# Two feature tiles of an up-projection by plain block products, other PSUM banks for the first output products, and a last column tile in two banks

## The chip, the cores and the metric

The kernel runs on one core of a Trainium2 chip. The metric is the device time of one execution in microseconds (us). Engines are named as in the profile: PE (TensorE, the matmuls), PEld (its weight loads), DVE (VectorE), ACT (ScalarE), POOL (GpSimd), SP (SyncE, which issues nearly all DMAs here).

## The reference

One decoder layer on 16 meta tokens and 1024 tokens, model width 1024, all in float32:

```
a   = rmsnorm(h) @ w_in                     # 1024 -> 3584: q, k, v of attention; q, f, i, g of HGRN
y1  = differential attention, 4 heads       # softmax(q1 k1) - lam * softmax(q2 k2), T5 bias, causal
y2  = HGRN2, 4 heads                        # gated linear recurrence, rmsnorm, silu gate
h   = h + rmsnorm([y1, y2] @ w_out)         # 1024 -> 1024
u   = causal conv3(rmsnorm(h) @ w_up) + b   # 1024 -> 2 * 2816
out = h + rmsnorm((gelu(u_gate) * u_up) @ w_down)
```

## The kernel before, in words

**Matmuls.** Every float32 matrix is split into a high part in the fast 32-bit format and the rest as a low part; a block product is three matmuls, high times high, high times low and low times high. A split is a cast on ACT and a subtraction on DVE or POOL.

**Order of work.** PE runs its instructions in the order in which the code writes them; generators that yield are interleaved by hand. On ACT, DVE, POOL and SP a scheduler sets the order by data readiness and its own costs, except where the code ties an instruction behind another (`tc.issue_after`, L1165 and others) or asks for program order. Once set, each engine works strictly in that order.

**Stages, with their place in the profile (us).** 0 to 66: norm and first projections. 66 to 538: heads in turn. Attention of head h is interleaved with the projections of HGRN head h, and HGRN head h with the attention projections of head h + 1. Beside them runs a side generator `wd_sums` (L254): first `down_sums`, which forms sums of down-projection weights, then `up_parts` (L214 to 252). It loads the four raw blocks of the up weights of feature tiles 1 and 2, forms the seven Strassen combinations with sums on POOL, splits each (cast on ACT, subtraction on POOL, L224), and stores both parts to a DRAM tensor `usc`: 28 stores of 256 KB.

538 to 602: the last HGRN head is interleaved with the first half of the output products, `out_first` (L1055). HGRN runs there as a recursion of levels; each level needs products of `mix` and `kr` from DVE before PE's next `pl` matmuls (L493). `out_first` goes through token blocks in the order `FIRST` (L960). Its first two blocks take their PSUM banks from `ps_in` (L1056), the pool that the input projections used until then; the last of these, `pi_hg`, is read by DVE to make `gate`. Rows of `w_out` are loaded (`wor`), cast (`woh`) and split (`wol`) by `load_wo`; `mix_split` splits `mix` into `mm` and stores it to `msc`.

602 to 667: second half of the output products, `py1`, a loop over nine token blocks in `order` (L1249 to 1290). In it `post_a` and `post_b` do norm and residual of a block and write its normed row `a2s`; `trans` (L1139) transposes it on PE two blocks later, and ACT copies it to `at2`. Half 0 of the tokens is split into quarter blocks (`t_split`) and Strassen sums (`t_sums`) on the way.

667 to 696: the transition (L1384 to 1425). Feature tile 0 goes through `plain_unit` (L1322): for each half of the tokens four quarters of 24 matmuls, that is two column blocks times two sides (gate `ug`, up `uu`), each over two inner blocks of four. The first two quarters of half 0 have a PSUM bank each, the third and fourth share one two-bank tile of attention's (`ps_s("pq2")`). Each quarter is read by an ACT copy. Then `gated` does convolution (`conv`, `c`), GELU and product.

696 to 1112: feature tiles 1 to 21 go through `unit` (L1342): seven Strassen products of 12 matmuls for each half of the tokens, PSUM accumulators `pa`, `pb`, `pc`. `prep(q)` (L1202) makes the weights of product q; for tiles 1 and 2 it loads them from `usc`, from tile 3 on it loads four raw blocks, sums on POOL and splits.

1112 to 1340: down-projection, in seven Strassen steps (`steps`, L1506 on), and the tail. The last column tile of the last product (m = 3) is cut into two halves of 256 in `last_sum_halves` (L1580), both in the bank `banks[4][3]`: matmuls of a half, addition to `x1`, squares; then rstd, two gains (`last_out`) and the output DMAs.

Of the kernel before, what the change touches and what calls it, by code (L numbers as in the profile page):

```python
# [18 lines left out]
P = 128  # L19
# [3 lines left out]
D = 1024  # L23
# [63 lines left out]
def layer_kernel(ctx: ExitStack, tc: tile.TileContext, x, meta, table, lbl, gpre, gpost, win,  # L87
# [56 lines left out]
    usc = dp.tile([2, 7, 2, P, 512], F32, tag="usc", name="usc")  # L144
# [22 lines left out]
    def rstd_of(dst, ss, n):  # L167
        A.activation(dst, ss, AF.Ln, bias=eps[: dst.shape[0]], scale=1.0 / n)
        A.activation(dst, dst, AF.Exp, scale=-0.5)
# [44 lines left out]
    def up_parts():  # L214
        b = [wsp.tile([P, 512], F32, tag="wd", name=f"up{n}") for n in range(5)]

        def load(ft, **what):
            for n, nm in what.items():
                with tc.issue_after(last_load[-1].ins):
                    SY.dma_start(b[int(n[1])], up_raw(ft, nm))  # L220

        def out(ft, j, src):
            A.copy(b[2].bitcast(F32R), src)
            G.tensor_tensor(b[3].bitcast(F32R), src, b[2], op=ALU.subtract)  # L224
            for l in range(2):
                with tc.issue_after(last_load[-1].ins):
                    SY.dma_start(usc[ft - 1, j, l], b[2 + l])

        load(1, b0="21", b1="22", b4="11")
        yield  # L230
        for ft in (1, 2):
            G.tensor_tensor(b[0], b[0], b[1], op=ALU.add)
            out(ft, 2, b[0])
            yield
            G.tensor_tensor(b[0], b[0], b[4], op=ALU.subtract)
            out(ft, 1, b[0])
            yield
            out(ft, 5, b[1])
            load(ft, b1="12")
            yield  # L240
            G.tensor_tensor(b[0], b[1], b[0], op=ALU.subtract)
            out(ft, 6, b[0])
            load(ft, b0="21")
            yield
            out(ft, 4, b[1])
            yield
            out(ft, 0, b[4])
            yield
            G.tensor_tensor(b[0], b[4], b[0], op=ALU.subtract)
            out(ft, 3, b[0])  # L250
            if ft == 1:
                load(2, b0="21", b1="22", b4="11")
            yield

    wd_sums = chain(down_sums(), up_parts())
# [799 lines left out]
    def out_first():  # L1055
        pys = [ps_in(f"py0_{i}") for i in FIRST[:2]]  # L1056
# [48 lines left out]
    a2t, xhs, a2s = {}, {}, []  # L1105
# [6 lines left out]
    def post_a(i, py):  # L1112
# [9 lines left out]
        V.scalar_tensor_tensor(xh[:r, 512:], tmp[:r], s1, xh[:r, 512:], ALU.mult, ALU.add)  # L1122

    def post_b(i):
# [8 lines left out]
        rstd_of(s2, s2, D)  # L1133
        V.scalar_tensor_tensor(a2[:r], xh[:r], s2, gfb[:r], ALU.mult, ALU.mult)
# [4 lines left out]
    def trans(i, bank=ps_m):  # L1139
# [4 lines left out]
        for half in range(2):  # L1144
# [4 lines left out]
            A.copy(at2[p][:, 4 * half:4 * half + 4, c:c + r], pt[:, : 4 * r].rearrange("p (k t) -> p k t", k=4))  # L1149
# [8 lines left out]
    def t_split(p, j, src, where, tag, step=None):  # L1158
# [5 lines left out]
        A.copy(hi[:, :, o:], src)  # L1164
        V.tensor_tensor(lo[:, :, o:], src, hi[:, :, o:].bitcast(F32), op=ALU.subtract)  # L1165
        if o:
            for a, b in zip((hi, lo), tt[p][0]):
                A.copy(a[:, :, :o], b[:, :, :o].bitcast(F32))
        tt[p][j] = (hi, lo)
# [20 lines left out]
    def load_raw4(ft, s):  # L1190
        raws.clear()
        for nm in ("11", "22", "21", "12"):
            raws[nm] = swp.tile([P, 512], F32, tag="ra", name=f"ra{s}_{nm}", bufs=5)
            with tc.issue_after(last_load[-1].ins):
                SY.dma_start(raws[nm], up_raw(ft, nm))
# [6 lines left out]
    def prep(q):  # L1202
# [7 lines left out]
        if ft < 3:  # L1210
            for l, t in enumerate((hi, lo)):
                with tc.issue_after(last_load[-1].ins):
                    SY.dma_start(t.bitcast(F32), usc[ft - 1, j, l])
            return
# [20 lines left out]
    def prep_plain():  # L1235
        load_raw4(0, "p")
        for j, nm in enumerate(("11", "12", "21", "22")):
# [11 lines left out]
    for n, i in enumerate(order):  # L1249
# [37 lines left out]
        if i == 8:  # L1287
            prep(8)
# [420 lines left out]
```

## Time and profile before

| what | us |
|---|---|
| median of 3 runs (lowest, highest) | 1345.74 (1342.92, 1347.78) |
| profiled execution | 1341.52 |
| its span, first to last instruction | 1339.7 |
| PE busy | 1286.7 (96%) |
| DVE, ACT, POOL busy | 916.5, 690.0, 424.1 |
| DMA moved | 168.29 MB |
| mean granted clock of TensorE | 0.997 |

Rows of the timeline read: start in us, duration in us, engine, line, operation, output <- inputs (buffer numbers left out), form, count; in brackets the idle time of the engine before it and what ended it. Line L54 stands for the helper that records all ACT and DVE operations, so tiles tell those apart. Rows of a window read: stretch, its length, then busy us and count for PE, PEld, DVE, ACT and POOL, the granted clock, the DMA share and GB/s. Rows of the waits read: engine, line, what it waited for, total us, times, longest.

### The profile page before, as it was taken

The page shows a single profiled execution, that of the slowest core. Times are in us where ns is not written, and L with a number is a line of the kernel's source. Part 1 is how long each engine was busy: PE and PEld are TensorE (multiplying, and loading weights), DVE is VectorE, ACT ScalarE, POOL GpSimd, SP SyncE. Part 2 cuts the span into 40 slices and gives each one's busy share as a digit, 9 for nine tenths or more (in the row PEclk, how much of TensorE's full clock was granted, in tenths as well). Part 3 has the DMA queues.
Part 4 walks back from the last instruction along what each step waited for, and adds up shares of the span by engine and source line. Part 5 has one row for each costly group of instructions (what it writes and reads, how often), then busy time and mean ns, then how long its engine had stood idle before and what let it go on. Part 6 is the DMA issues. An engine that isn't in the chain of part 4 may idle for free.

```text
span 1339.7 us, 26379 instructions
## 1 busy us (share of the span) xinstructions
PE 1286.7 (96%) x10182; PEld 1184.5 (88%) x10182; DVE 916.5 (68%) x1595; ACT 690.0 (52%) x1669; POOL 424.1 (32%) x335
## 2 busy tenths in 40 slices
PE   6999999999998999999989999999999999999997
PEld 5898899989987989777789999999999998888886
DVE  7565657574758465744896777777787776697586
ACT  7465346534653575535674454454454444554453
POOL 3211212021225430103223566666657640010020
PEclk9999999999999999999999999999999999999999
DMA  6331333143314420825844222223222225965353
GB/s 215 108 133 52 104 116 110 48 128 103 103 60 143 134 95 16 261 88 196 268 161 154 95 74 82 83 77 114 80 88 71 80 80 182 336 205 165 95 205 118
DMA packets 92580, 168.29 MB, mean 126 GB/s; under 512 B 10483, under 2 KB 20755, under 8 KB 92454
## 3 DMA queue, kind: packets, MB, share of 16 engines
q1 hardware_dynamic: 92454, 166.60, 37.4%
q8 instruction: 80, 1.31, 0.4%
q14 instruction: 46, 0.38, 0.1%
HBM read 120.56 MB, written 46.01 MB: 124 GB/s over the span
## 4 chain that ended last, share of the span: by engine, by line
PE 53%; DVE 6%; ACT 3%; issue 2%; DMA 2%; POOL 1%; SPq 0%; DVEq 0%; ACTq 0%; POOLq 0%
PE pd L1527 5%; PE pd L1528 5%; PE pd L1526 5%; PE pb L1355 4%; PE pb L1356 4%; PE pb L1357 4%; PE pa L1355 2%; PE pa L1356 2%; PE pa L1357 2%; PE pc L1356 2%; PE pc L1355 2%; PE pc L1357 2%; PE py L1012 2%; PE py L1016 2%; PE py L1014 2%
## 5 line engine op out<-in xcount | busy, mean ns | idle before, releaser
L1355 PE MATMUL pb<-t,uh 128*128 128x258 f32 (+1 forms) x504 | 142.6, 283 | 2.1 <-DVE u L54 1.9
L1357 PE MATMUL pb<-t,ul 128*128 128x258 f32 (+1 forms) x504 | 141.4, 281 | 0.0
L1356 PE MATMUL pb<-t,uh 128*128 128x258 f32 (+1 forms) x504 | 141.3, 280 | 0.0
L1526 PE MATMUL pd<-wh,gh 128*128 128x512 f32 (+1 forms) x307 | 120.9, 394 | 1.0 <-DVE x L54 1.0
L1527 PE MATMUL pd<-wl,gh 128*128 128x512 f32 (+1 forms) x307 | 121.1, 394 | 0.3 <-DVE wl L54 0.2
L1528 PE MATMUL pd<-wh,gl 128*128 128x512 f32 (+1 forms) x307 | 121.0, 394 | 0.0
L1319 POOL TENSOR_TENSOR c<-c,c 128x512 f32<-128x512 f32 x44 | 63.0, 1432 | 150.5 <-ACT c L54 129.0
L54 DVE SCALAR_TENSOR_TENSOR c<-uu,cwt,c 128x512 f32<-128x512 f32 x88 | 93.6, 1063 | 20.8 <-ACT c L54 20.1
L1355 PEld LDWEIGHTS pb<-t,uh 128*128 128x128 f32 x504 | 95.1, 189 | 3.3 <-DVE u L54 3.1
L1357 PEld LDWEIGHTS pb<-t,ul 128*128 128x128 f32 x504 | 95.6, 190 | 0.0
L1356 PEld LDWEIGHTS pb<-t,uh 128*128 128x128 f32 x504 | 94.9, 188 | 0.0
L1355 PE MATMUL pa<-t,uh 128*128 128x258 f32 (+1 forms) x336 | 94.7, 282 | 0.0
L1356 PE MATMUL pa<-t,uh 128*128 128x258 f32 (+1 forms) x336 | 94.4, 281 | 0.0
L1357 PE MATMUL pc<-t,ul 128*128 128x256 f32 x336 | 94.3, 281 | 0.0
L1355 PE MATMUL pc<-t,uh 128*128 128x256 f32 x336 | 94.3, 281 | 0.0
L1356 PE MATMUL pc<-t,uh 128*128 128x256 f32 x336 | 94.3, 281 | 0.0
L1357 PE MATMUL pa<-t,ul 128*128 128x258 f32 (+1 forms) x336 | 94.1, 280 | 0.0
L54 DVE SCALAR_TENSOR_TENSOR c<-ug,cwt,c 128x512 f32<-128x512 f32 x88 | 84.5, 960 | 1.8 <-ACT c L54 1.1
L1527 PEld LDWEIGHTS pd<-wl,gh 128*128 128x128 f32 x307 | 57.9, 189 | 14.2 <-DVE wl L54 1.1
L1526 PEld LDWEIGHTS pd<-wh,gh 128*128 128x128 f32 x307 | 57.9, 189 | 14.2 <-DVE x L54 1.2
L1528 PEld LDWEIGHTS pd<-wh,gl 128*128 128x128 f32 x307 | 57.9, 189 | 13.1
L54 ACT ACTIVATE pb<-S,ast 128x528 f32<-128x528 f32 (+7 forms) x72 | 46.5, 647 | 39.0 <-DVE ast L54 38.9
(417 smaller groups left out, 4165.8 us busy)
## 6 DMA issues: line engine op xcount, KB each, us to landing
ra<-in_wup_dram SPq DMA_DIRECT2D x76, 256.0 KB, 2.7
wd<-in_wdown_dram SPq DMA_DIRECT2D x44, 256.0 KB, 4.4
tsc<-wd SPq DMA_DIRECT2D x44, 256.0 KB, 3.1
gsc<-c SPq DMA_DIRECT2D x44, 256.0 KB, 2.0
wi<-tsc SPq DMA_DIRECT2D x44, 256.0 KB, 2.7
gi<-gsc SPq DMA_DIRECT2D x33, 256.0 KB, 4.0
wi<-in_wdown_dram SPq DMA_DIRECT2D x33, 256.0 KB, 3.4
usc<-up SPq DMA_DIRECT2D x28, 256.0 KB, 2.1
```

Of the source, the lines that this page charges most:

```text
L54: ins = call(*args, **kw)
L1012: T.matmul(py[:r], mh[:, j, :r], hi, start=(first and j == 0), stop=False)
L1014: T.matmul(py[:r], mh[:, j, :r], lo, start=False, stop=False)
L1016: T.matmul(py[:r], ml[:, j, :r], hi, start=False, stop=(last and k == k1 - 1))
L1319: G.tensor_tensor(cg, cg, cu, op=ALU.mult)
L1355: T.matmul(pt, hi[:, s], th[:, k], start=(first and k == 0), stop=False, skip_group_check=True)
L1356: T.matmul(pt, hi[:, s], tl[:, k], start=False, stop=False, skip_group_check=True)
L1357: T.matmul(pt, lo[:, s], th[:, k], start=False, stop=(k == 3), skip_group_check=True)
L1526: T.matmul(py, gh[:, s], wh, start=(k == 0 and pr not in (3, 7)), stop=False, skip_group_check=True)
L1527: T.matmul(py, gh[:, s], wl, start=False, stop=False, skip_group_check=True)
L1528: T.matmul(py, gl[:, s], wh, start=False, stop=(k == NH - 1), skip_group_check=True)
```

## The change

It has three parts.

1. `up_parts` and `usc` are gone. Feature tile 1 goes through `plain_unit` too, on weights that `prep_plain(1, ...)` loads and splits near the end of the `py1` loop (splits on POOL). Tile 2 is prepared in place from raw blocks, whose loads are tied behind the first store of unit 0. The transition is written in a new order: splits and sums are moved, and `behind(...)` ties some to marked instructions (`xh`, `rstd`, `turned`, `hi`, `lo`). In the `py1` loop `trans` moves from the third part to the fourth.
2. The first two blocks of `out_first` take banks of attention's pool `ps_s` in place of `ps_in`.
3. The last column tile has two banks, one for each half, and all its steps run as two 256-wide products; the gain of block 2 moves between the halves, and its output DMA goes out in two halves.

```diff
@@ up weights split ahead @@
-    def up_parts():
-        b = [wsp.tile([P, 512], F32, tag="wd", name=f"up{n}") for n in range(5)]
...
-    wd_sums = chain(down_sums(), up_parts())
+    wd_sums = down_sums()
@@ out_first @@
-        pys = [ps_in(f"py0_{i}") for i in FIRST[:2]]
+        pys = [ps_s(f"py0_{i}")[:, 0] for i in FIRST[:2]]
@@ ties @@
+    @contextmanager
+    def behind(*names):
+        with ExitStack() as st:
+            for nm in names:
+                st.enter_context(tc.issue_after(marks[nm].ins))
+            yield
@@ load_raw4 @@
-            with tc.issue_after(last_load[-1].ins):
+            with tc.issue_after(marks["store"].ins if "store" in marks else last_load[-1].ins):
@@ prep @@
-        if ft < 3:
-            for l, t in enumerate((hi, lo)):
-                with tc.issue_after(last_load[-1].ins):
-                    SY.dma_start(t.bitcast(F32), usc[ft - 1, j, l])
-            return
@@ plain weights @@
-    def prep_plain():
-        load_raw4(0, "p")
...
+    def prep_plain(ft, names):
+        for nm in names:
+            raw = swp.tile([P, 512], F32, tag="ra", name=f"rap{ft}_{nm}", bufs=5)
+            with tc.issue_after(last_load[-1].ins):
+                SY.dma_start(raw, up_raw(ft, nm))
+            where = wp if nm[1] == "1" else swp
+            hi, lo = (where.tile([P, 512], F32R, tag=t, name=f"u{t[1]}{ft}_{nm}", bufs=4) for t in ("wh", "wl"))
+            split(hi, lo, raw, G)
+            plain[ft, nm] = (hi, lo)
@@ py1 loop @@
-                if n >= 2:
-                    trans(order[n - 2])
+            if c == 3 and n >= 2:
+                trans(order[n - 2])
...
-            prep(7)
-        if i == 8:
-            prep(8)
+        if i == 3:
+            prep_plain(1, ("12", "22"))
         post_a(i, py)
     post_b(8)
+    with behind("rstd"):
+        prep_plain(1, ("11", "21"))
@@ transition @@
-    p0 = plain_unit(0, lambda nm: free.pop(0))
+    p0 = plain_unit(0, 0, lambda nm: free.pop(0))
+    next(p0)
+    with behind("xh"):
+        t_split(1, 0, quarter(1, 0), tp, "t1_0")
     next(p0)
     trans(7)
-    t_split(0, 1, sum_quarter(0, 1), tp, "t0_1", 264)
-    t_split(0, 2, sum_quarter(0, 2), tp, "t0_2")
-    t_split(1, 0, quarter(1, 0), tp, "t1_0")
-    prep(9)
     next(p0)
-    t_split(1, 4, quarter(1, 4), tp, "t1_4")
-    next(p0)
-    prep(10)
+    with behind("xh", "rstd"):
+        t_split(1, 4, quarter(1, 4), tp, "t1_4")
     next(p0)
     trans(8)
     t_split(1, 7, quarter(1, 7), tp, "t1_5")
     t_split(1, 6, quarter(1, 6), mxp, "mix2", 384)
-    t_split(0, 3, sum_quarter(0, 3), tp, "t0_3")
-    t_split(0, 5, sum_quarter(0, 5), mxp, "mix0", 272)
+    next(p0)
+    with behind("hi", "lo"):
+        t_split(0, 1, sum_quarter(0, 1), tp, "t0_1", 264)
+        t_split(0, 2, sum_quarter(0, 2), tp, "t0_2")
+        t_split(0, 3, sum_quarter(0, 3), tp, "t0_3")
...
+    p0 = plain_unit(1, 0, ps_b)
+    for j in range(4):
+        next(p0)
...
+    p1 = plain_unit(1, 1, ps_b)
...
-    for ft in range(1, NF):
+    for ft in range(2, NF):
@@ last column tile @@
-        py, wh, wl = banks[pr][m][:, c0:c1], wh[:, c0:c1], wl[:, c0:c1]
+        py, wh, wl = (banks[pr][m + c0 // 256] if c1 - c0 < 512 else banks[pr][m])[:, :c1 - c0], wh[:, c0:c1], wl[:, c0:c1]
...
-            V.tensor_tensor(c[:, h], py[:, h], c[:, h], op=ALU.add)
+            if n:
+                last_out(m - 1, 0)
+            V.tensor_tensor(c[:, h], pys[n][:, :256], c[:, h], op=ALU.add)
...
-            mms(i, m)
+            if (pr, m) == (4, 3):
+                mms(i, m, 0, 256)
+                mms(i, m, 256, 512)
+            else:
+                mms(i, m)
```

DVE at the first output products, before: `wol` are low parts of rows of `w_out` for the first half, `wl_0` and `wl_1` rows 0 and 1 for the second half, `mm_0` and `mm_4` low parts of `mix` blocks, `mix` with `f` the products of HGRN level 1.

```order
719 L54 TENSOR_TENSOR wol_6_6455<-wor_6_6452,woh_6_6454 128x512
720 L54 TENSOR_TENSOR wol_7_6461<-wor_7_6458,woh_7_6460 128x512
721 L54 TENSOR_TENSOR mm_0_6558<-mix_101,mm_0_6558 128x512
722 L54 TENSOR_TENSOR mix_101<-mix_101,f_5515 128x384
723 L54 TENSOR_TENSOR mix_100<-mix_100,f_5515 128x272
724 L54 TENSOR_TENSOR mix_102<-mix_102,f_5515 128x384
725 L54 TENSOR_TENSOR a_6488<-pd_6491,ident_729 128x256
726 L54 TENSOR_TENSOR am<-pd_6491,ident_729 16x16
727 L54 TENSOR_TENSOR wl_0_6617<-wor_0_6614,wh_0_6616 128x512
728 L54 TENSOR_TENSOR wl_1_6623<-wor_1_6620,wh_1_6622 128x512
729 L54 TENSOR_TENSOR mm_4_6627<-mix_101,mm_4_6627 128x384
730 L54 TENSOR_TENSOR wol_2_6747<-wor_2_6744,woh_2_6746 128x512
```

The same place in the changed kernel (tile numbers are shifted):

```order
719 L53 TENSOR_TENSOR wol_6_6375<-wor_6_6372,woh_6_6374 128x512
720 L53 TENSOR_TENSOR mm_0_6478<-mix_100,mm_0_6478 128x512
721 L53 TENSOR_TENSOR wol_7_6381<-wor_7_6378,woh_7_6380 128x512
722 L53 TENSOR_TENSOR mix_99<-mix_99,f_5477 128x272
723 L53 TENSOR_TENSOR mix_100<-mix_100,f_5477 128x384
724 L53 TENSOR_TENSOR mix_101<-mix_101,f_5477 128x384
725 L53 TENSOR_TENSOR a_6408<-pd_6411,ident_728 128x256
726 L53 TENSOR_TENSOR am<-pd_6411,ident_728 16x16
727 L53 TENSOR_TENSOR mm_4_6547<-mix_100,mm_4_6547 128x384
728 L53 TENSOR_TENSOR wl_0_6537<-wor_0_6534,wh_0_6536 128x512
729 L53 TENSOR_TENSOR mix_100<-mix_100,f_5477 128x192
730 L53 TENSOR_TENSOR mm_0_6609<-mix_100,mm_0_6609 128x512
```

`mm_0` now stands ahead of `wol_7`, and `wl_1` and `wol_2` have moved behind the products of the next level.

SP's queue of DMAs at the same place, before: `wor` are loads of rows of `w_out`, `msc` stores of split `mix` blocks, `mp` loads of them.

```order
226 L972 DMA wor_0_6614<-in_wout_dram 128x512
227 L972 DMA wor_1_6620<-in_wout_dram 128x512
228 L972 DMA wor_2_6744<-in_wout_dram 128x512
229 L1050 DMA mp_0_6939<-msc 128x512
230 L1050 DMA mp_1_6941<-msc 128x512
231 L1003 DMA msc<-mm_0_6558 256x1x256 x2
```

And in the changed kernel:

```order
188 L929 DMA wor_0_6534<-in_wout_dram 128x512
189 L960 DMA msc<-mm_0_6478 256x1x256 x2
190 L929 DMA wor_1_6540<-in_wout_dram 128x512
191 L960 DMA msc<-mm_4_6547 256x1x256
192 L960 DMA msc<-mm_4_6547 256x1x128
193 L929 DMA wor_2_6664<-in_wout_dram 128x512
```

The loads of rows 1 and 2 of the second half stand behind stores of `mm_0` and `mm_4`, which wait for DVE.

ACT at the transition, before: `t_` are casts of quarter blocks, `at_1` with `pa` the copies of transposed blocks, `ug` and `uu` with `pq` the evacuations of quarters, `c` the convolution and GELU.

```order
763 L54 ACTIVATE at_1_7234,ssy<-xh_7732 128x8x128
764 L54 CAST t_3_8016<-at_0_7238 128x1024
765 L54 ACTIVATE ssy<-ssy,eps 128x1
766 L54 ACTIVATE ssy<-ssy 128x1
767 L54 COPY ug_0_7862<-pq_7859 128x258
768 L54 COPY uu_0_7863<-pq_7860 128x258
769 L54 COPY ug_0_7862<-pq_7861 128x256
770 L54 ACTIVATE c_0_0_8156<-ug_0_7862,cbt,cwt 128x512
771 L54 COPY ug_1_8030<-ug_0_7862 128x2
772 L54 CAST t_5_8019<-at_0_7238 128x4x258
773 L54 ACT_TABLE_LOAD
774 L54 ACTIVATE c_0_0_8156<-c_0_0_8156 128x512
```

And in the changed kernel, up to the evacuation of the fourth quarter:

```order
741 L53 COPY at_1_7154<-pa_7_0_7853 128x4x128
742 L53 ACTIVATE ssy<-ssy,eps 128x1
743 L53 COPY at_1_7154<-pa_7_1_7859 128x4x128
744 L53 ACTIVATE ssy<-ssy 128x1
745 L53 CAST uh_11_7770<-rap_11_7768 128x512
746 L53 CAST uh_21_7776<-rap_21_7774 128x512
747 L53 CAST t_4_7890<-at_1_7154 128x1024
748 L53 COPY ug_0_7798<-pq_7795 128x258
749 L53 COPY uu_0_7799<-pq_7796 128x258
750 L53 COPY ug_0_7798<-pq_7797 128x256
751 L53 COPY uu_0_7799<-pq_7797 128x256
```

The fourth quarter's evacuation (`uu_0<-pq_7861` before, `uu_0<-pq_7797` now) stood behind the table load and GELU and stands ahead of them now. The copies of block 7 and the casts of `uh_11`, `uh_21` and `t_4` stand ahead of the evacuations of the first three quarters.

More of the change, by code (lines that the diff above doesn't have):

```diff
@@ L1 @@
 import math
[L2 to L3 removed]
+from contextlib import contextmanager, ExitStack, nullcontext
 import concourse.bass as bass
@@ L1338, in plain_unit @@
                 yield
-        gated(0, p, *us)
+        with behind("turned"):
+            gated(ft, p, *us)
         yield
```

110 lines of the change are left out of this document (37 added, 73 removed).

## The prediction

> **What bounds the kernel now.** I read the head of the page first, then the chain that ended last, then the waits of PE, and then the stretches in which those waits lie.
>
> ```profile
> span 1339.7 us, 26379 instructions
> PE 1286.7 (96%) x10182; PEld 1184.5 (88%) x10182; DVE 916.5 (68%) x1595; ACT 690.0 (52%) x1669; POOL 424.1 (32%) x335
> PE 53%; DVE 6%; ACT 3%; issue 2%; DMA 2%; POOL 1%; SPq 0%; DVEq 0%; ACTq 0%; POOLq 0%
> ```
>
> TensorE (PE) is busy 96% of the span, and no other engine comes near. Whatever the change is worth must therefore come out of the 53 us in which PE did nothing, out of stretches at a low granted clock, or out of the number of matmuls. The waits of PE say who ends its idle time (total us, times, longest):
>
> ```profile
> PE pl L493 <- DVE mix L54: 7.7, 8, 2.7
> PE pa L1148 <- DVE a2s L54: 3.2, 3, 2.0
> PE py L1012 <- DVE gate L54: 2.6, 2, 2.1
> PE pq L1334 <- ACT uu L54: 2.0, 1, 2.0
> PE pq L1334 <- ACT ug L54: 0.5, 1, 0.5
> PE pd L1526 <- DVE x L54: 1.0, 1, 1.0
> ```
>
> These six rows name every wait that the change touches: HGRN levels that wait for VectorE (DVE), the first output products that wait for a PSUM bank (gate), the transition between output projection and up-projection (a2s, ug, uu), and the last column tile (x). They hold 17 us together, and the change reaches only a part.
>
> **D. Weights no longer split ahead (up_parts goes).** Its DVE, ACT and POOL work lay beside attention and HGRN. The windows compare each stretch "attention projections beside an HGRN head" of heads 0, 1 and 2, and then the three later stretches "HGRN projections beside attention" (length, then busy us of PE, PEld, DVE, ACT, POOL):
>
> ```profile
> 142.90:195.70 52.80, 50.59 (x733) 47.49 (x732) 34.93 (x79) 22.23 (x63) 9.56 (x12) 1.00 0.35 108
> 272.39:326.55 54.16, 51.08 (x733) 47.65 (x732) 34.97 (x79) 22.24 (x63) 10.29 (x12) 1.00 0.33 105
> 403.50:460.80 57.30, 51.06 (x732) 47.47 (x732) 37.75 (x71) 27.12 (x72) 27.49 (x25) 1.00 0.42 137
> 195.70:272.39 76.69, 74.22 (x506) 71.24 (x505) 44.91 (x104) 44.57 (x134) 12.59 (x11) 1.00 0.27 90
> 326.55:403.50 76.95, 74.66 (x506) 71.22 (x506) 46.01 (x104) 45.10 (x135) 16.94 (x14) 1.00 0.29 97
> 460.80:538.57 77.77, 74.38 (x505) 71.16 (x504) 45.67 (x103) 48.44 (x145) 17.81 (x14) 1.00 0.24 79
> ```
>
> Head 2 does the same work as head 0 and 1 plus most of up_parts, and takes 3.14 us longer than head 1 and 4.50 longer than head 0. POOL has 17 us more there, ACT 5. The last stretch, with the rest of up_parts, is 0.82 longer than the one before it and 1.08 longer than the first. Why DVE suffers is seen from one operation of the HGRN head, in the window of head 2 and then of head 1, and from what ran beside it (count, busy us, mean ns):
>
> ```profile
> L224 POOL TENSOR_TENSOR up<-up,up 128x512 fp32r<-128x512 f32 x9 | 12.6, 1399 | 11.8 <-ACT up L54 8.9 <-DMA usc<-up 3.0
> L54 DVE TENSOR_TENSOR kr<-kr,tt 128x520 f32<-128x520 f32 x2 | 3.4, 1680 | 0.0
> ...
> L54 DVE TENSOR_TENSOR kr<-kr,tt 128x520 f32<-128x520 f32 x2 | 1.4, 700 | 0.0
> ```
>
> The same DVE product took 1680 ns beside the splits and 700 without, and the HGRN levels on PE wait for exactly these products (the row "pl <- DVE mix", 7.7 us). With up_parts gone head 2 should look like heads 0 and 1. The gain is 3.1 to 4.5 there plus 0.8 to 1.1 behind. I take the means, 3.8 + 0.95, and round down to **−4.4** because a part of up_parts also ran beside stretches with slack; bounds −3.0 and −5.6. The weights' loads and 28 stores of 256 KB went with it; DMA had room there (share 0.42), so they add nothing.
>
> [...]
>
> **A. First output products in attention's banks.** At 538 us PE changes from the last projection to these products. Rows of PE, ACT, DVE, then the DMA loads of the output weights, and the window:
>
> ```profile
> 542.85 0.50 PE L1012 MATMUL py<-wh,mm 128*128 128x512 f32 x1 [2.10 <-DVE gate L54]
> 545.29 0.63 PE L1014 MATMUL py<-wol,mm 128*128 128x512 f32 x1
> 545.72 0.63 PE L1016 MATMUL py<-woh,mm 128*128 128x512 f32 x1
> 552.79 0.70 PE L493 MATMUL pl<-mix,kr 128*32 128x16 f32 x62
> ...
> 556.43 0.71 PE L493 MATMUL pl<-mix,kr 128*32 128x16 f32 x62
> ...
> 544.19 1.27 ACT L54 CAST woh<-wor 128x512 fp32r<-128x512 f32 x2 [2.16 <-DMA wor<-in_wout_dram]
> ...
> 544.84 1.34 DVE L54 TENSOR_TENSOR wol<-wor,woh 128x512 fp32r<-128x512 f32 x2 [2.05 <-ACT woh L54]
> ...
> DMA to landing us min/median/max: 2.4/4.2/5.6
> ...
> 548.00:564.00 16.00, 16.00 (x334) 12.42 (x333) 13.43 (x34) 7.60 (x15) 3.59 (x5) 1.00 0.93 297
> ```
>
> Both waits for gate (2.6 us) are waits for a bank of the projections, and go. Behind the longer one the matmuls start 0.43 us apart (545.29 to 545.72) where this width otherwise starts every 0.23 (twice the 20.00 us / 172 of the 256-wide ones in the window under B); some eight of them at the half clock lose 1.7 us. The upper bound of A is 2.6 + 1.7 = 4.3.
>
> What is late next is the split of wo row 6 (ready at 545.5: the first of two DVE splits of 0.67 us from 544.84). PE reaches its first product with it after 30 matmuls of 0.23 and the first HGRN level, at 538.6 + 7.6 = 546.2, so it just fits. Level 1 of HGRN (552.79 before) would start at 548.4, once DVE has done row 6, one mm low part, row 7 and three products of mix. That is the full 4.3. But the order on DVE and on the loads' queue moves too: the stores of mix now stand ahead of the second half's weight loads, and wl_1 and wol_2 stand behind them on DVE. A load takes 4.2 us to land in a stretch whose DMA share is 0.93. Going through DVE's order with these durations I get level 2 at 553 (before 556.4), and, each later level a few tenths longer than before, a lead that shrinks to 2.6 by the fifth. I take **−2.6**, bounds −4.3 and 0.
>
> [...] Here a gap of 2.10 us, with 0.5 us just ahead of it, was followed by half-clock spacing, while the one of 2.7 us in the row of pl was not (clock 1.00 in its window). [...]
>
> **B. The transition.** The first matmul of unit 0, the three waits, and the windows of a plain unit (96 matmuls) and of a Strassen tile (168; x172 includes neighbours):
>
> ```profile
> 666.79 0.28 PE L1334 MATMUL pq<-t,uh 128*128 128x258 f32 x1
> ...
> 685.03 0.38 PE L1334 MATMUL pq<-t,uh 128*128 128x256 f32 x1 [1.99 <-ACT uu L54]
> ...
> 685.00:696.00 11.00, 10.97 (x96) 10.97 (x97) 10.49 (x10) 9.26 (x14) 0.00 (x0) 1.00 0.24 64
> 696.00:716.00 20.00, 20.00 (x172) 19.94 (x171) 12.31 (x21) 6.06 (x13) 2.96 (x2) 1.00 0.76 267
> ...
> 670.48 1.28 DVE L54 SCALAR_TENSOR_TENSOR a2s<-xh,ssy,gfb 128x1024 f32<-128x1024 f32 x1
> ...
> 677.01 2.32 DVE L54 SCALAR_TENSOR_TENSOR a2s<-xh,ssy,gfb 128x1024 f32<-128x1024 f32 x1
> ...
> 678.67 0.37 ACT L54 COPY ug<-pq 128x256 f32<-128x256 f32 x1 [1.18 <-PE pq L1336]
> ...
> 684.87 1.08 ACT L54 COPY at<-pa 128x512 f32<-128x512 f32 x2
> 685.83 2.96 ACT L54 CAST t<-at 128x1024 fp32r<-128x1024 f32 x3
> ```
>
> Tile 1 by plain products costs 24 more matmuls of 0.116 us (20.00 / 172): **+2.8**. Three waits stand against it: 2.0 for a2s of block 7, 0.5 for ug, 2.0 for uu, 4.5 together. The first goes because sums and splits of half 0 no longer stand on DVE ahead of a2s; the third because the table load and GELU no longer stand on ACT ahead of the evacuation. The bound without waits is 2.8 − 4.5 = −1.7.
>
> I do not think all goes. Quarters 3 and 4 still share one PSUM tile, so quarter 4 waits for the evacuation of quarter 3. On ACT there now stand ahead of it: two copies of the transposes of block 7 (1.08), the casts of the new weights 11 and 21 (2 x 0.63 by the cast row of A), a cast of t1_4 (1.0, a third of 2.96), and the evacuations of quarters 1 and 2 (2 x 0.37, as the one at 678.67). Counted from unit 0's start, quarters 1 and 2 end at 5.6, the transposes at 6.4, quarter 3 at 9.2. ACT starts the copies at 6.4 at the earliest and has quarter 3 out at 6.4 + 1.1 + 1.3 + 1.0 + 0.7 + 0.4 = 10.9. Quarter 4 waits 1.7. So B is 2.8 − 4.5 + 1.7 = **0.0**. Bounds: −1.7 (ACT free in time), +1.5 (block 6's transposes wait longer, since three sums now stand on DVE ahead of its a2s, or the POOL splits stretch a2s as 677.01 against 670.48: 2.32 for 1.28). Cover: tile 2's weights are loaded after the first store of unit 0 and needed, by my count, some 20 us later, when both units of tile 1 are done (2 x 11.0); a load, a cast and a split are 4.2 + 0.6 + 0.7 of that. If that cover were gone, a first split late by 3 us would cost 3.
>
> **C. The last column tile.** PE's last wait, DVE's last gain, and the last two output DMAs:
>
> ```profile
> 1331.03 0.38 PE L1526 MATMUL pd<-wh,gh 128*128 128x256 f32 x1 [0.96 <-DVE x L54]
> ...
> 1335.41 0.75 DVE L54 SCALAR_TENSOR_TENSOR hh<-x,ssd,hh 128x512 f32<-128x512 f32 x1
> 1335.52 0.99 SPq L1602 DMA_DIRECT2D out_dram<-hh  x2
> ```
>
> With a bank of its own the second half no longer waits for the first half to be read: 0.96 goes. The chain behind (sum, squares, rstd, two gains, two DMAs) keeps its length; only one gain of block 2 changes places, into DVE time in which it waited for PE. The first steps of this tile run as two 256-wide matmuls each, seven steps of three pairs, at 2 x 0.116 for 0.23: +0.1 at most. **−0.9**, bounds 0 and −1.4.
>
> **Sum.** −4.4 − 2.6 + 0.0 − 0.9 = −7.9. The profiled run took 1341.52 (span 1339.7 and 1.8 around it), which is 0.3% under the median of the three runs, 1345.74. I carry the difference over: 1341.5 − 7.9 = 1333.6 on the scale of that run, 1345.7 − 7.9 = **1337.8** on that of the medians, which is what I predict.
>
> **Rivals.**
>
> 1. *The waits only change places.* The stretch of A is bound by its DMA (share 0.93), so that an earlier start buys nothing once the loads are behind the stores (A = −0.5), and ACT's new queue keeps PE waiting in B while block 6 waits too (B = +1.5). D at its lower bound and C stay: −3.0 − 0.5 + 1.5 − 0.9 = −2.9, 1342.8. For it speaks the moved order of SP; against it that PE is the busy engine of 548 to 564 (16.00 of 16.00). Chance 0.15.
> 2. *All terms at their good end.* −5.6 − 4.3 − 1.7 − 1.4 = −13.0, 1332.7. For it: level 1 does start 4.3 earlier in my replay. Against: wl_1's load. Chance 0.18.
> 3. *Slower: weight loads of the second half one level late.* If DVE reaches wl_1 or wol_2 before the load has landed, everything behind it on DVE stands, the level's kr and mix products too, and so PE. The loop is then closed: a mix low part on DVE (0.7) lets the store go, the store lets the load go (1.2 for both issues), it lands 4.2 later, cast and split take 0.63 + 0.67, the level's products 1.7: 9.1 us a level, where levels lie 3.6 apart (552.79 to 556.43). Three such levels lose 16 us, and with the −7.9 that is +8, 1354. It decides from the point at which a load lands more than about 2 us behind DVE. Chance 0.06.
> 4. *The change does not remove its waits.* The banks of S are still held when the first products want them, or quarter 4's wait brings the half clock with it: A = 0, B = +1.5, with D and C as forecast −3.8, 1341.9. Chance 0.08.
>
> The forecast, within its bounds, keeps 0.53.
>
> **How the numbers follow.** A measurement here can tell about 0.3% (4 us) from no change: faster is below 1341.7, slower above 1349.8. The forecast and rival 2 are faster, rivals 1 and 4 mostly within 4 us, rival 3 slower. The forecast's bounds lie nearly all below 1341.7; of rivals 1 and 4, which stand just above it, I count a third as faster. That gives 0.53 + 0.18 + 0.08 = 0.79 faster, 0.15 the same, 0.06 slower. The range takes rival 2 with 1.5 us below it and reaches up to rivals 1 and 4 with 1 us above: 1331 to 1344; rival 3 and some of the extremes stay out.
>
> **What would show it.** Right: head 2's stretch near 53.5 us with kr products at 700 ns; no wait of py for gate, no 0.43 us spacing near 544, level 1 of the last head at 548.4 less what D took ahead of it; a wait of pq for ug of 1.5 to 2 us; no wait of pd for x at the end. Wrong: head 2 still near 57 us (then POOL was not the cause), levels of the last HGRN head more than 5 us apart, a wait of pa for a2s of 2 us, or a wait for tile 2's first weights.

## The result, and the profile after

The changed kernel takes 1336.8 us (median of 6 runs, 1335.2 to 1338.1) against 1345.6 of the kernel before: ratio 0.9937, 95% interval [0.9922, 0.9952], faster by 0.6%. The forecast was 1337.8. Timed again beside the last experiments it took 1338.1, ratio 0.9945 [0.9927, 0.9963]. One execution of experiment 9, the one that was profiled, ran at a mean clock of 0.56 and took 2092.9 us; it is left out.

The page of the changed kernel and the waits of PE (lines have moved by about 40):

```profile
span 1335.8 us, 26319 instructions
PE 1288.8 (96%) x10227; PEld 1191.1 (89%) x10227; DVE 914.6 (68%) x1589; ACT 690.3 (52%) x1670; POOL 414.1 (31%) x324
...
PE pb L1319 <- DVE u L53: 8.1, 4, 6.3
PE pl L450 <- DVE mix L53: 4.9, 7, 1.1
PE pa L1112 <- DVE a2s L53: 2.4, 1, 2.4
PE pq L1297 <- ACT ug L53: 1.4, 1, 1.4
```

PE is busy 2.1 us longer (24 more matmuls) and idle 6 us less (47.0 in place of 53.0). The waits for gate, for uu and for x at the end are gone. The wait of `pl` for mix has fallen from 7.7 to 4.9. One wait is new and large: 6.3 us of `pb` for `u`, in the first Strassen tile.

Where the time went is read from the start of each stage's first matmul. The lengths come from one profile of before and two of the changed kernel, in us; each is a difference of two start times:

| stage | before | changed | changed, second profile |
|---|---|---|---|
| start to attention of head 2 (the same instructions) | 326.55 | 329.05 | 326.32 |
| attention 2 to first output product (D) | 212.53 | 201.63 | 201.39 |
| first output product to HGRN level 5 (A) | 28.87 | 26.03 | 26.29 |
| level 5 to first plain unit | 98.84 | 100.20 | 100.35 |
| first plain unit to tile 2 (B) | 49.06 | 48.31 | 48.31 |
| tile 2 | 19.85 | 28.41 | 28.55 |
| tile 3 to the last matmul (C) | 597.01 | 595.59 | 595.65 |

The first row is a gauge: 330 us of the same instructions take 2.7 us more or less in two profiles of one kernel. In these two profiles the other rows repeat within 0.3 us, but that is not so for all of them in more profiles. The runs of experiments 2, 5 to 8, 10 and 11 have the same instructions in the same order up to level 5: over all nine profiles D is 201.4 to 202.5, and A 26.0 to 28.8. With the old banks A is 28.9 (before) and 30.3 (experiment 4). So the row of D can be taken as it stands, and the row of A only as a mean of several profiles.

The rows behind the first sum to −6.0 and −5.6, while the medians differ by 8.8. The profiled execution of before took 1341.5 against a median of 1345.6, so 2 to 3 us of the gain in time have no place in the table.

D, in the windows of the changed kernel: head 0 and head 1 beside attention projections, attention of head 2 beside HGRN projections, head 2, then the last projections beside attention:

```profile
144.07:196.86 52.79, 50.56 (x732) 47.47 (x732) 34.90 (x79) 22.23 (x63) 9.56 (x12) 1.00 0.33 108
...
274.07:329.05 54.98, 52.37 (x733) 49.17 (x733) 35.07 (x79) 22.24 (x63) 10.41 (x12) 0.97 0.32 104
...
329.05:404.77 75.72, 73.89 (x505) 71.20 (x505) 44.57 (x104) 44.59 (x134) 12.58 (x11) 1.00 0.26 88
404.77:455.99 51.22, 50.57 (x732) 47.54 (x732) 29.19 (x71) 22.23 (x63) 9.56 (x12) 1.00 0.12 37
455.99:530.68 74.69, 73.34 (x506) 71.24 (x506) 44.40 (x102) 47.25 (x140) 9.77 (x8) 1.00 0.12 38
```

Head 2 did not come down to 53.5 as forecast but to 51.22, below heads 0 and 1; the last stretch fell from 77.77 to 74.69. The third busy time (DVE) says why: 29.19 in head 2, 34.90 in head 0. The group behind the difference, in head 0's window of the changed kernel:

```profile
L53 DVE TENSOR_TENSOR wd<-wd,wd 128x512 f32<-128x512 f32 x8 | 5.6, 697 | 2.3 <-DMA wd<-in_wdown_dram 1.4 <-DMA wr_hi<-in_win_dram 0.8
```

Heads 0 and 1 carried eight subtractions of `down_sums` each, 5.6 us of DVE. They were no free baseline: PE's waits in head 0 and in head 2 of the changed kernel, the second of which has one row,

```profile
PE pl L450 <- DVE mix L53: 1.6, 2, 1.0
PE pi_dv L231 <- ACT k L53: 0.5, 1, 0.5
```

```profile
PE pi_dv L231 <- ACT k L53: 0.5, 1, 0.5
```

differ by the 1.6 us by which head 0 is longer. Head 2 before had these, and its `kr` products, 1680 ns before, are short now:

```profile
PE pl L493 <- DVE mix L54: 4.2, 4, 2.7
PE pl L487 <- DVE kr L54: 1.0, 1, 1.0
```

```profile
L53 DVE TENSOR_TENSOR kr<-kr,tt 128x520 f32<-128x520 f32 x2 | 1.4, 698 | 0.0
```

So 5.2 of the 6.1 us in head 2 are waits of the HGRN levels for DVE. In that window of before, eight DVE products took 1.35 to 1.79 us that take 0.29 to 0.74 now, and an operation of POOL overlaps each of them in the trace. No run takes away POOL's part of `up_parts` alone; that POOL and not the transfers slowed DVE rests on these rows.

A: the first output product follows the last projection 0.18 us later, and the levels start at

```profile
530.68 0.40 PE L969 MATMUL py<-wh,mm 128*128 128x512 f32 x1
...
540.48 0.29 PE L450 MATMUL pl<-mix,kr 128*32 128x16 f32 x13
...
556.71 0.27 PE L450 MATMUL pl<-mix,kr 128*32 128x16 f32 x9
```

Against the first product, level 1 comes at +9.80 (before 552.79 − 539.08 = +13.71) and level 5 at +26.03 (before +28.87): a lead of 3.9 that shrinks to 2.8, plus the first wait of 0.5. The lead is lost at one place, between levels 2 and 3. ACT's cast of row 2 of the second half (`woh`) waits there for its load, and DVE stands idle until the cast is done, with the products of level 3 behind it:

```profile
546.15 0.62 ACT L53 CAST woh<-wor 128x512 fp32r<-128x512 f32 x1 [2.63 <-DMA wor<-in_wout_dram]
546.81 0.69 DVE L53 TENSOR_TENSOR wol<-wor,woh 128x512 fp32r<-128x512 f32 x1 [2.37 <-ACT woh L53]
```

Level 3 comes 4.8 us behind level 2 here, against 3.7 before. In the eleven profiles with the new banks DVE's idle time at this place is 2.2 to 3.6 us, and level 3 comes 4.6 to 6.0 us behind level 2, in nine of them more than 5.

The new wait, on PE and then on DVE ahead of it:

```profile
720.18 0.58 PE L1319 MATMUL pb<-t,uh 128*128 128x256 f32 x1 [6.31 <-DVE u L53]
720.57 0.41 PE L1320 MATMUL pb<-t,uh 128*128 128x256 f32 x1
720.78 0.41 PE L1321 MATMUL pb<-t,ul 128*128 128x256 f32 x1
720.99 0.42 PE L1319 MATMUL pb<-t,uh 128*128 128x256 f32 x1
```

```profile
697.78 3.48 DVE L53 SCALAR_TENSOR_TENSOR c<-ug,cwt,c 128x512 f32<-128x512 f32 x2
701.18 2.32 DVE L53 TENSOR_TENSOR t<-at,t 128x1032 fp32r<-128x1032 f32 x1
703.42 2.58 DVE L53 SCALAR_TENSOR_TENSOR c<-uu,cwt,c 128x512 f32<-128x512 f32 x2
705.92 5.69 DVE L53 TENSOR_TENSOR t<-at,t 128x1024 fp32r<-128x1024 f32 x3
711.53 1.78 DVE L53 TENSOR_TENSOR ul<-ra,uh 128x512 fp32r<-128x512 f32 x1
713.23 2.55 DVE L53 SCALAR_TENSOR_TENSOR c<-ug,cwt,c 128x512 f32<-128x512 f32 x2
...
719.71 0.42 DVE L53 TENSOR_TENSOR u<-pb,x 128x256 f32<-128x256 f32 x1
```

PE stands still from 713.9 and then starts matmuls every 0.21 us in place of 0.116 for 4 us: the half clock (granted clock 0.50 from 717.81 to 724.64), about 2 us more. DVE is busy with one gap of 0.27 us: convolutions of tiles 0 and 1, five token splits, three subtractions for tile 2's weights, and only then the addition that frees a PSUM bank. A split of 1.22 us takes up to 2.32 there.

C: DVE at the end of the changed kernel,

```profile
1329.09 0.75 DVE L53 SCALAR_TENSOR_TENSOR hh<-hh,ssd,hh 128x512 f32<-128x512 f32 x1
1329.75 0.42 DVE L53 TENSOR_TENSOR x<-pd,x 128x256 f32<-128x256 f32 x1
...
1331.97 0.74 DVE L53 SCALAR_TENSOR_TENSOR hh<-x,ssd,hh 128x512 f32<-128x512 f32 x1
```

No wait of PE for x is left in this stage. The last addition now starts 0.5 us behind PE's last matmul, held up by the gain of block 2 (0.04 before), but the last gain ends 3.5 us behind that matmul (1329.2), as before (1336.2 behind 1332.7).

### The profile page after: what moved, and what is told of

Its sections match the earlier page's. It is cut to its first block, busy times and chain, and to the rows that moved or that the text cites. A ratio compares the mean times of both kernels' runs of the same rounds, so it can differ in the third digit from the quotient of the medians.

```text
span 1335.8 us, 26319 instructions
## 1 busy us (share of the span) xinstructions
PE 1288.8 (96%) x10227; PEld 1191.1 (89%) x10227; DVE 914.6 (68%) x1589; ACT 690.3 (52%) x1670; POOL 414.1 (31%) x324
## 5 line engine op out<-in xcount | busy, mean ns | idle before, releaser
L1319 PE MATMUL pb<-t,uh 128*128 128x258 f32 (+1 forms) x480 | 136.9, 285 | 8.1 <-DVE u L53 8.1
L1320 PE MATMUL pb<-t,uh 128*128 128x258 f32 (+1 forms) x480 | 135.6, 283 | 0.0
L1321 PE MATMUL pb<-t,ul 128*128 128x258 f32 (+1 forms) x480 | 135.6, 283 | 0.0
L1280 POOL TENSOR_TENSOR c<-c,c 128x512 f32<-128x512 f32 x44 | 66.9, 1520 | 132.0 <-ACT c L53 123.6
L1319 PEld LDWEIGHTS pb<-t,uh 128*128 128x128 f32 x480 | 91.6, 191 | 9.2 <-DVE u L53 8.9
L1321 PEld LDWEIGHTS pb<-t,ul 128*128 128x128 f32 x480 | 92.0, 192 | 0.0
L1320 PEld LDWEIGHTS pb<-t,uh 128*128 128x128 f32 x480 | 91.4, 190 | 0.0
L1319 PE MATMUL pa<-t,uh 128*128 128x258 f32 (+1 forms) x320 | 90.2, 282 | 0.0
L1320 PE MATMUL pa<-t,uh 128*128 128x258 f32 (+1 forms) x320 | 89.9, 281 | 0.0
L1321 PE MATMUL pc<-t,ul 128*128 128x256 f32 x320 | 89.9, 281 | 0.0
L1319 PE MATMUL pc<-t,uh 128*128 128x256 f32 x320 | 89.9, 281 | 0.0
L1320 PE MATMUL pc<-t,uh 128*128 128x256 f32 x320 | 89.9, 281 | 0.0
L1321 PE MATMUL pa<-t,ul 128*128 128x258 f32 (+1 forms) x320 | 89.7, 280 | 0.0
L155 POOL TENSOR_TENSOR ul<-ws,uh 128x512 fp32r<-128x512 f32 x40 | 58.2, 1454 | 35.4 <-ACT uh L53 31.6
```

What stands on the lines that cost most here:

```text
L155: (eng or G).tensor_tensor(lo, raw, hi.bitcast(F32), op=ALU.subtract)
L1280: G.tensor_tensor(cg, cg, cu, op=ALU.mult)
L1319: T.matmul(pt, hi[:, s], th[:, k], start=(first and k == 0), stop=False, skip_group_check=True)
L1320: T.matmul(pt, hi[:, s], tl[:, k], start=False, stop=False, skip_group_check=True)
L1321: T.matmul(pt, lo[:, s], th[:, k], start=False, stop=(k == 3), skip_group_check=True)
```

## Experiments

Ratios are against the kernel before, timed beside each run; the changed kernel has 0.9937 and 0.9945. Runs are compared with the changed kernel by these ratios or by medians. Stretches of the experiments are, like those of the table, from one profile each. The diffs are excerpts; `...` marks what is left out.

**1. up_parts back.** The changed kernel with the removed generator (its text as before, not shown) running, its results unread:

```diff
-    wd_sums = down_sums()
+    wd_sums = chain(down_sums(), up_parts())
```

> The changed kernel with up_parts back beside attention and HGRN: loads, sums, casts, splits and the 28 stores run as before, but nothing reads what they store; everything else is as changed (time 1336.8). Forecast: up_parts costs 4.4 us, so about 1341. Reading of the two profiles (heads 2 and 3 together are 9 to 11 us shorter than before, of which the same instructions ahead of them vary by 2.5): 8 to 10 us, so about 1345 to 1347. If the shorter stretches come from something else, 1337.

Measured: 1349.4 us, ratio 1.0031 [1.0016, 1.0045]. The difference to the changed kernel is 0.9% or 12 us, above both expectations (the upper one, 8 to 10 us, lies at the edge of the intervals). Head 2 and the last stretch in this run:

```profile
405.48:463.06 57.58, 51.10 (x732) 47.48 (x732) 37.79 (x71) 27.12 (x72) 27.46 (x25) 1.00 0.41 136
463.06:540.56 77.50, 74.18 (x505) 71.33 (x505) 45.49 (x102) 48.27 (x144) 17.80 (x14) 1.00 0.23 78
```

They are 6.4 and 2.8 us longer than in the changed kernel, and 11.1 are lost by the first plain unit (667.97 against 656.91), of which 1.9 come between head 3 and there or ahead of head 2. This settles that D is the removal and what it is worth: without it, the rest of the change is slower than before by 0.3%. PE's waits in head 2 are back as they were before: 4.2 us for mix and 1.0 for kr.

**2. Tile 2 with casts only.**

```diff
+        if ft == 2:
+            if j == 0:
+                load_raw4(ft, ft)
+            made[q] = (hi, hi)
+            A.copy(hi, raws[("11", "22", "21", "12")[j % 4]])
+            return
```

> The changed kernel with the preparation of tile 2 cut down: each of its seven products takes one raw block, cast on ACT, as high and as low part, so the POOL sums and the five DVE or POOL subtractions for tile 2 are left out and the output is not the layer's; loads, casts and matmuls stay. If preparing tile 2 in place causes the new wait of 6.3 us at 720 and the half clock behind it (2.1 us), both go: about -8 us, 1328.5. If the wait comes from the convolutions and the quarter splits that stand on DVE anyway, more than 4 us of it stay: above 1333.

Measured: 1335.1 us, ratio 0.9925 [0.9911, 0.9939]; only 1 to 3 us better. The wait fell from 6.31 to 1.57, but another came at tile 3:

```profile
718.00 0.39 PE L1325 MATMUL pb<-t,uh 128*128 128x256 f32 x1 [1.57 <-DVE u L53]
...
744.53 0.40 PE L1325 MATMUL pb<-t,uh 128*128 128x258 f32 x1 [1.90 <-DVE u L53]
```

The run leaves out seven low parts (four on DVE, three on POOL), not the five expected, and four sums. From the first plain unit to tile 3 it takes 69.8 us against 76.7, so most of the 8.4 goes with tile 2's sums and subtractions. But 2.4 return one tile later (22.3 us for tile 3 in place of 19.9): what is left of DVE's queue still holds up an addition. Neither expectation came whole. By these stages the run gains 4.5, by the time 1 to 3; in its one profile the rows ahead of the first plain unit are 2.6 longer, which no edit explains.

**3. Banks alone**, on the kernel before:

```diff
-        pys = [ps_in(f"py0_{i}") for i in FIRST[:2]]
+        pys = [ps_s(f"py0_{i}")[:, 0] for i in FIRST[:2]]
```

> The kernel before with one line changed: the first two blocks of the first output products in attention's banks. Forecast: -2.6 us (first levels 4 us earlier, then 2.6), so about 1343. If the transfers bound the stretch, no change (1345.5). Full gain of waits and clock: -4.3, 1341.

Measured: 1341.8 us, ratio 0.9978 [0.9964, 0.9991], −3.0 us with an interval of −4.8 to −1.2. The waits for gate are gone and the clock over the first products is 1.00 (the window of this run from 540 on):

```profile
540.00:546.00 6.00, 6.00 (x90) 4.73 (x89) 4.13 (x10) 4.37 (x10) 0.00 (x0) 1.00 0.91 289
```

**4. The tail alone**, on the kernel before (last hunk of the diff and the order of the gains).

> The kernel before with only the last column tile in two banks and its gains and output DMAs as in the change. Forecast: -0.9 us (the wait of 0.96 goes, 0.1 comes for the narrower steps), so about 1344.6; if the chain behind the matmuls takes up the lead, no change.

Measured: 1344.9 us, ratio 0.9995 [0.9981, 1.0009]. The time can't tell −0.9 from nothing. In the profile the wait of `pd` is gone and the stage from the first down-projection matmul to the last matmul takes 215.5 us against 216.9 (216.9 also in experiment 3, which has the old tail, and 215.8 in both profiles of the changed kernel).

**5. Three plain tiles.**

```diff
-    prep(14)
-    prep(15)
+    prep_plain(2, ("11", "12", "21", "22"))
...
+    p0 = plain_unit(2, 0, ps_b)
...
+    p1 = plain_unit(2, 1, ps_b)
...
-    for ft in range(2, NF):
+    for ft in range(3, NF):
```

> The changed kernel with tile 2 by plain products too (its four blocks loaded and split like those of tile 1), tile 3 the first Strassen tile, prepared behind it; token splits 1 to 3 and 5 of the second half and the last split of the first move back by one tile. Theory: the new wait at tile 2 comes from a backlog on DVE, which tile 2's sums and subtractions prolong; 24 more matmuls cost 2.8, and 22 us of PE work without Strassen sums let DVE catch up, so the wait and the half clock (8.4 together) go: -5.6, about 1331. Rival: the backlog only moves with the first Strassen tile, and the wait comes at tile 3: +2.8, about 1339.6.

Measured: 1333.4 us, ratio 0.9905 [0.9886, 0.9924], 3.4 to 5.4 us under the changed kernel, by medians and by ratios. The waits list keeps only the small waits for `u` that both kernels had:

```profile
PE pb L1319 <- DVE u L53: 1.8, 3, 0.7
```

From the first plain unit to tile 3 it takes 70.4 us in place of 76.7, −6.3 with 2.8 us of added matmuls in it. The rival falls: with the same preparation one tile later, the wait does not come back (1.8 us of small waits in place of 8.1).

**6. Two tiles for the third and fourth quarter.**

```diff
-    both = ps_s("pq2")
-    free += [both[:, 0], both[:, 1]]
+    free += [ps_s("pq2")[:, 0], ps_s("pq3")[:, 0]]
```

> The changed kernel with the third and fourth quarter of the first plain unit in two tiles of attention's banks in place of one, so that quarter 4 doesn't wait for the evacuation of quarter 3 (1.38 us in the profile). If PE is the bound of the transition: -1.4, 1335.4. If DVE is (backlog from 657 to 720 us), the wait at tile 2 grows by what PE wins here: 0, 1336.8.

Measured: 1336.4 us, ratio 0.9929 [0.9911, 0.9947], no difference that the intervals tell. The wait of 1.4 is gone, and the one at tile 2 is 6.1. By its one profile the stretch up to tile 3 is 1.9 shorter, which speaks for the first alternative; the time alone decides neither.

**7. Tile 2's sums and low parts on DVE**: `w_sum` and `split` with V for ft = 2.

> The changed kernel with the sums and all low parts of tile 2's weights on DVE, none on POOL (seven more DVE operations of 0.7, 4.9 us). Theory: POOL's sums and splits hold up DVE by more than that (DVE operations of 0.74 and 1.22 us take 1.66 and 2.32 there, some 8 us together), so the wait at tile 2 shrinks: -2 to -4, about 1334. Rival: DVE is bound by its own work, then +4.9, about 1341.5.

Measured: 1338.7 us, ratio 0.9952 [0.9933, 0.9970]. Neither came: the wait at tile 2 shrank from 6.3 to 4.6 with 0.8 behind it, and the stretch from the first plain unit to tile 3 is 76.1 against 76.7. In that stretch DVE is busy 58.7 us in place of 61.9, in spite of the seven operations more, so POOL did hold it up; but only 0.6 us of that reach PE, and the time shows no gain.

**8. Transposes one part earlier**: `c == 2` in place of `c == 3`.

> The changed kernel with the transposes of the py1 loop at the third part again, as before the change. On PE block 6's transposes then wait for a2s about 1.4 us longer (six 512-wide matmuls fewer ahead of them, against 2.37 now), and the first plain unit starts about that much later. If PE is the bound: +1.4, 1338.2. If DVE is: 0, since the wait at tile 2 shrinks by as much.

Measured: 1338.0 us, ratio 0.9945 [0.9929, 0.9962], no change in time. My reason was wrong, though: the wait of block 6 for a2s did not grow but nearly vanished, and two others grew. By the rows of DVE, block 6's `a2s` stands ahead of the last sum of half 0 in this run and behind it in the changed kernel.

```profile
PE pb L1319 <- DVE u L53: 8.6, 4, 6.7
PE pq L1297 <- ACT ug L53: 2.3, 1, 2.3
...
PE pa L1112 <- DVE a2s L53: 0.6, 2, 0.4
```

PE is 1.5 us quicker from level 5 to the first plain unit and 2.6 slower from there to tile 3, at quarter 4 (where the half clock follows the wait: granted clock 0.72 from 666 to 672) and at tile 2. The time lies between the two expectations and decides neither.

**9. No subtractions in down_sums.**

```diff
-            b["t3"] = wsp.tile([P, 512], F32, tag="wd", name=f"wd3_{k}")
...
-                V.tensor_tensor(b[d], b[p_], b[q_], op=ALU.subtract)
...
-                    SY.dma_start(tsc[j][P * k: P * (k + 1)], b[d])
+                    SY.dma_start(tsc[j][P * k: P * (k + 1)], b[p_])
```

> The changed kernel without the four DVE subtractions a step of down_sums; raw blocks are stored in place of their differences, so the sums for the down-projection are left out and the output is not the layer's. Theory: the forecast measured head 2 beside up_parts against heads 0 and 1, which were no free baseline, since each carried 8 of these subtractions (5.6 us of DVE). Then heads 0 and 1 come down to head 2 now (51.2, from 52.8 and 55.0), the stretches of attention come down too, and the whole falls by 6 to 9 us, to about 1329. If the subtractions lie in free DVE time, the stretches stay and the time is 1336.8.

Measured: 1324.7 to 1329.0 us in three runs, ratio 0.9858 [0.9834, 0.9882], about 11 us under the changed kernel and more than expected. The 44 subtractions (32.9 us of DVE in the changed kernel's profile, eight in each head and attention stretch up to attention of head 2) cost nearly as much as `up_parts`; the loads and stores of `down_sums` stay, and one of its buffers goes. That heads 0 and 1 are the stretches that shrink is not shown.

**10 and 11. Three plain tiles with two tiles for the quarters, and then with the sums of half 0 later.** Run 10 joins the edits of 5 and 6; run 11 adds this:

```diff
-        if i == 7:
-            t_sums(0)
...
+    with behind("a2"):
+        t_sums(0)
     post_b(8)
```

> Three plain tiles (1333.4) and the third and fourth quarter in two tiles. With the wait at tile 2 gone, PE is the bound behind the transition, so what was worth nothing alone now counts: -1.0 to -1.4, about 1332.2. If another wait takes its place: 1333.4.

> The kernel of the run above, with the token sums of half 0 tied behind a2s of block 7, so that they no longer stand on DVE ahead of a2s of block 6. The wait of PE for a2s (2.25 us) goes to some 0.3, and the sums fall into DVE's idle time behind it: -1.5 to -2, about 1330.5. If the sums now delay a2s of block 8 or the splits of half 0, the gain is lost there: 1332.2 or more.

Measured: 1331.6 us, ratio 0.9892 [0.9872, 0.9911], and 1329.3 us, ratio 0.9880 [0.9859, 0.9902]. Each step is near its expectation, though neighbours in this chain have overlapping intervals. The last is 0.6% under the changed kernel timed beside it (0.9945 [0.9927, 0.9963]) and beats both kernels clearly. Its waits list has no row for a2s or ug any more, and from level 5 to the first plain unit it takes 97.5 us (101.2 in run 10, 100.2 in the changed kernel).

**12. The changed kernel again.**

> The changed kernel itself, beside the others on one chip: 1336.8, and a second profile of it, which shows how far the same instructions vary from run to run.

Measured: 1338.1 us, ratio 0.9945 [0.9927, 0.9963]. Its profile is the last column of the table of stages.

## Why the prediction was right, and where it was wrong

The total was right within 1 us, and largely by luck: D gave 6 to 8 us more than forecast and B cost 9 us where nothing was forecast, so two errors as large as the whole change nearly cancelled.

- **D, −4.4 forecast.** The mechanism held as far as the rows show it: the `kr` products took 1680 ns beside POOL's splits and take 698 now, and 5.2 us of waits of the HGRN levels for DVE went with that. The size was −10.4 by the stages (10.9 less the first wait of 0.5, which is A's) and about −12 by time (experiment 1). The step that failed is "head 2 should look like heads 0 and 1": those carried `down_sums`, and so did the earlier attention stretches that the last one was held against. That is 4.4 of the 6.0 us missing in the stages (head 2 gave 6.1 in place of 3.8, the last stretch 3.1 in place of 0.95). Another 1.2 come from attention of head 2 (76.95 to 75.72), where up_parts had begun (POOL 16.94 us, now 12.58) and which the sum left out; 0.4 is the rounding down. The rows of before could have shown it: DVE was busy 34.9 us in heads 0 and 1 and 37.75 in head 2, which I took for the same work. Head 2 alone needs 29.2, so up_parts had stretched it by 8.6.
- **A, −2.6 forecast.** The size is right as far as the runs can tell: alone −3.0 by time, and by the row of A a mean of 27.3 in eleven profiles with the new banks against 28.9 and 30.3 with the old, with the first wait of 0.5 on top. The course is right too: a lead of 3.9 at level 1 and 2.8 at level 5, against 4.3 and 2.6. But the lead was to shrink by a few tenths a level, and it is lost at one level, by a late load. Rival 1's transfers took a part, not the whole.
- **B, 0.0 forecast.** The waits that were named are as forecast: uu gone, 1.4 us for ug (1.7 forecast), and block 6's a2s at 2.4 in place of 0.8, which was the bad bound and one of the signs of being wrong (experiment 11 takes it away by moving the sums behind it). The plain stage itself is 0.75 shorter. What failed is the sentence on cover, that tile 2's weights have 20 us for a load, a cast and a split. PE did not wait for these weights, but I counted their latency and not the queue: DVE had no gap from 697.8 to 716.9, and the addition that frees a PSUM bank stood at its end. That cost 8.6 us, 6.3 of wait and about 2 of half clock. With 1.4 in the py1 loop and −0.75, B was about +9. Experiments 2 and 5 show it: with less on DVE, or with more time for it, the wait goes.
- **C, −0.9 forecast.** −1.1 to −1.4 by the stage of the down-projection (215.5 to 215.8 in three profiles, 216.9 in two with the old tail); the time of the tail alone can't tell it from zero.
- **Rivals.** Rival 3 (weight loads a level late) came in its first step: DVE stood 2.4 us for row 2 of the second half, and level 3 came late. Its loop did not close: the levels behind lie 3.6 to 4.0 us apart in the changed kernel's profile, 5.0 to 5.3 once more in three other runs, and not 9.1. Its sign, levels more than 5 us apart, is met in nine of eleven profiles, at a cost of 1 to 2.3 us and not 16. Rival 4's half clock did come, but at tile 2. The mechanism of rival 1, "The waits only change places", was right in kind, and the place was missed.

At tile 2 the split at 701.18 (128x1032) took 2.32 us, with a POOL sum beside it from 700.67 to 702.41, and the one at 715.69 (128x1024) took 1.22 us, with POOL busy 0.04 us from 714.40 to 717.81. But experiment 7 (1338.7 us) shows that taking POOL away there gains nothing in time when the same work comes to DVE.

## What to carry to other kernels

Before one stage is measured against another as "without the side work", compare the busy time of every engine in both: a baseline may carry side work of its own. When work is deferred into a busy stage, count the whole queue of the engine that does it up to the operation that frees the next buffer, not the latency of the one job. And compare profiles by stages, with a stretch of unchanged instructions as a gauge, and take more than two of them: here the totals of two profiles of one kernel differed by 2.4 us while their changed stages agreed within 0.3, but over nine profiles of the same instructions one of these stages spread over 2.8.

## What the runs showed of the hardware that was not expected

Idle gaps of PE of nearly one length were sometimes followed by the half clock and sometimes not. Here is the same wait for a2s in the changed kernel and in experiment 10, with two windows each (the granted clock is the third number from the end):

```profile
654.59 0.33 PE L1112 MATMUL pa<-ident,a2s 128*128 128x128 f32 x1 [2.37 <-DVE a2s L53]
...
652.96:656.37 3.41, 1.78 (x12) 1.65 (x13) 3.41 (x4) 1.08 (x2) 0.50 (x1) 1.00 0.21 34
656.37:659.79 3.42, 3.42 (x28) 3.29 (x27) 0.50 (x2) 3.27 (x9) 0.00 (x0) 1.00 0.68 278
```

```profile
655.82 0.44 PE L1112 MATMUL pa<-ident,a2s 128*128 128x128 f32 x2 [2.38 <-DVE a2s L53]
...
653.33:656.74 3.41, 1.03 (x10) 0.93 (x9) 3.41 (x4) 0.41 (x2) 1.35 (x1) 1.00 0.47 174
656.74:660.15 3.41, 3.41 (x12) 2.83 (x11) 0.94 (x2) 2.54 (x5) 0.00 (x0) 0.50 0.79 294
```

2.37 us cost only itself; 2.38 us brought a clock of 0.50 over the next 3.41 us, by estimate half of that, 1.7 us, more. The stretches are not chosen freely; they follow the clock records of the traces. In the changed kernel the half clock lasts 3.41 us from 294.56 and 6.83 us from 717.81, in before 3.41 us from 543.72, and the two starts in the changed kernel lie 423.25 us apart, 124 times 3.413. Divide each profile into steps of 3.413 us that meet the start of a half clock in it. Experiment 10's gap then lies in one step, in which PE was idle 2.38 us; the changed kernel's gap is divided between two, and the fuller has 1.63. The gap of 2.7 us in the row of pl, which the prediction held up as one without half clock, is divided too: 1.55 and 1.17 in before. In experiment 4, where the same gap lies with 2.37 us in one step, the half clock follows:

```profile
424.25:427.67 3.42, 1.87 (x12) 1.55 (x10) 3.39 (x4) 1.00 (x2) 3.42 (x4) 1.00 0.24 89
427.67:431.08 3.41, 2.24 (x73) 2.21 (x74) 2.53 (x6) 1.22 (x3) 0.96 (x1) 1.00 0.71 235
```

```profile
424.28:427.69 3.41, 1.04 (x7) 0.72 (x5) 3.41 (x3) 0.96 (x2) 3.41 (x3) 1.00 0.33 91
427.69:431.10 3.41, 3.06 (x70) 3.02 (x71) 2.51 (x9) 1.66 (x4) 0.14 (x1) 0.50 0.60 220
```

In before and in the changed kernel, divided in this way from 20 to 1320 us, three steps at full clock were followed by the half clock, and PE was idle in them for 2.10 us (before, from 540.31), 1.73 and 3.41 us (changed, from 291.15 and 714.40). In the steps at full clock that were followed by the full clock PE was idle for 1.81 us at most (before, from 670.01). So the idle time of a step does not part the two cases at 1.73 and 1.81 us. That the part of a gap inside one step is what counts is an estimate from these rows, where idle time goes by the recorded matmuls; no run was made to test it.
